# Weight tiles moved 64 bytes further on, and the second MLP's token shift taken out

## The chip, the cores and the metric

The kernel runs on one core of one Trainium2 chip. The metric is the device time of one execution in microseconds (us). Three runs of the kernel before gave 1178.79, 1179.38 and 1179.67 us, a median of 1179.38 us. All times below are of that kernel unless said otherwise.

A matmul on TensorE (PE) has two operands in SBUF. The *stationary* one (`lhsT`, 128 columns) is loaded into the array by a weight load (engine PEld in the profile); the *moving* one (`rhs`, here 256 or 512 columns) is then streamed through. The weight load of the next matmul runs while the present one streams.

## The reference

Two layers of a small diffusion transformer over 256 image tokens (x) and 256 context tokens (ctx), width 1024, all in float32. Layer 0 mixes tokens by retention (4 heads, keys 256 wide, values 512 wide, forward and backward), layer 1 by neighbourhood attention (32 heads of 32). Each is followed by a gated residual with a layer norm, and by an MLP:

```python
def sq_relu_mlp(h, w1, w2):
    return jnp.square(jax.nn.relu(h @ w1)) @ w2

h = x * (1.0 + sc2) + sh2
x = layer_norm(DN_ALPHA * x + g2 * sq_relu_mlp(h, mlp_w1[i], mlp_w2[i]), ln_g[i, 1], ln_b[i, 1])
```

`w1` is 1024x4096 and `w2` 4096x1024. In layer 0 the MLP is applied to image and context tokens, in layer 1 (the last) to the 256 image tokens alone. Shifts, scales and gates come from `c` and `c_ctx` by the 1024x6144 matrices `ada_w`.

## The kernel before, in words

**Three products for one.** Each float32 operand is split in a high part (rounded to the type that PE multiplies at one pass, `float32r`) and a low part (the rest). A product of two such pairs is three matmuls into one PSUM bank: high by high, high by low, low by high (`mm3`, line 174). So PE runs three matmuls per block, and nearly all of them have one of the weights' tiles, `hi` or `lo`, as an operand.

**Weights.** The list `specs` holds 228 blocks of weights (mostly 512 KB) in the order of use. `fetch` (line 255) loads a block into a `raw` tile with a DMA on SP's queue, ScalarE (ACT) rounds it into a `hi` tile, and VectorE (DVE) subtracts to make `lo`. `hi` tiles come from pool `hip` and `lo` tiles from pool `lop`, five of each. One block lies instead in an arena slot (tile `hilo`), and two in the pool of scratch tiles, `scp`.

**Tokens.** The normalised, scaled and shifted tokens stand transposed in `hTh` and `hTl` (high and low), 128 partitions by 8 blocks of 512 columns, image tokens first. `hs(k, a, b)` (line 583) gives columns a to b of block k of both.

**Which operand moves.** The places differ in what is loaded and what is streamed:

- Weights stationary, tokens moving. With 512 columns: retention's queries and keys (PSUM tile `pq`), the first MLP's first product (`p`, `mm1`, line 1254), part of the attention's keys (`pn`). With 256 columns: the first MLP's first two column blocks, where image and context tokens are taken apart (`p`); the attention's queries and the other part of its keys (`pn`, lines 1445 and 1475); and the second MLP's first product (`p`, `mm1` called at line 2072).
- Weights moving, the other operand stationary. With 512 columns: values (`pv`, `pnv`), gates (`pg`), the two output projections (`pw`, `pnw`), and the second products of both MLPs (`p<-hi,hid`, `p<-lo,hid`). With 256 columns: a quarter of the second MLP's second product (`mm2b`, line 2094), part of `pnw`, and the opening of the second MLP, where the tokens of one half come before the other's (`tok_part`, line 1975, PSUM tile `p1t`).
- No weights' tile at all: retention scores (`pS`), score times value (`po`), attention scores, transposes.

**Where the tiles lie.** SBUF is handed out pool by pool in the order in which the pools are opened (lines 136 to 142). By the built program, every large tile of the kernel before starts at 160 modulo 512 bytes of its partition: `hTh` at 40608, `raw` from 81568, `hi` from 97952, `lo` from 118432, scratch from 138912, the arena from 155296. Blocks within a tile are multiples of 512 bytes apart, so each operand of a matmul starts at 160 too, with one exception: in the second MLP the tokens are written, and read, 112 columns (448 bytes) further on in each block (`AT = 7 * LINE`, `LINE` being 16 floats). There the tokens' operand starts at 160 + 448 = 608, which is 96 modulo 512.

**What sets the order.** A scheduler orders the instructions of an engine, save where the code pins them (`keep_in_program_order`). All instructions are recorded through one helper, so the profile gives line 84 for nearly all of them; the tile names tell the place.

Of the kernel before, what the change touches and what calls it, by code (L numbers as in the profile page):

```python
# [10 lines left out]
F32 = mybir.dt.float32  # L11
# [6 lines left out]
P = 128  # L18
# [18 lines left out]
LINE = 16  # L37
# [67 lines left out]
def kernel(  # L105
# [27 lines left out]
    ec = ctx.enter_context  # L133
# [2 lines left out]
    smp = ec(tc.tile_pool(name="smp", bufs=4))  # L136
    cpool = ec(tc.tile_pool(name="cpool", bufs=1))
    rawp = ec(tc.tile_pool(name="rawp", bufs=4))
    hip = ec(tc.tile_pool(name="hip", bufs=WB))
    lop = ec(tc.tile_pool(name="lop", bufs=WB))  # L140
    scp = ec(tc.tile_pool(name="scp", bufs=8))
    arena = ec(tc.tile_pool(name="arena", bufs=1))
    dram = ec(tc.tile_pool(name="dram", bufs=1, space=DRAM))
    psp = ec(tc.tile_pool(name="psp", bufs=8, space=PSUM))

# [10 lines left out]
    def bank(s="ps"):  # L156
        return psp.tile([P, 512], F32, tag="ps", name=nm(s))

    def slot(i, shape, dt, s):

        return arena.tile(shape, dt, tag=f"s{i}", name=nm(s))
# [4 lines left out]
    def tsl(t):  # L166
        return slice(t * P, (t + 1) * P)
# [6 lines left out]
    def mm3(o, a, b, start, stop):  # L174
        (ah, al), (bh, bl) = a, b
        pe.matmul(o, lhsT=ah, rhs=bh, start=start, stop=False)
        pe.matmul(o, lhsT=ah, rhs=bl, start=False, stop=False)
        pe.matmul(o, lhsT=al, rhs=bh, start=False, stop=stop)
# [76 lines left out]
    def fetch(n, in_scratch=False, at=None):  # L255

        for src, k, ncol in specs[len(units) : len(units) + max(n, 0)]:
            raw = rawp.tile([P, k, ncol], F32, tag="raw", name=nm("raw"))
            sp.dma_start(out=raw[:], in_=src.rearrange("(k p) n -> p k n", p=P))
            if in_scratch or len(units) in scratch_units:  # L260
                hi, lo = Rows([scr("hi", F32R) for _ in range(k)]), Rows([scr("lo", F32R) for _ in range(k)])
                for i in range(k):
                    act.copy(out=hi[:, i, :], in_=raw[:, i, :])
                    pending.append((lo[:, i, :], raw[:, i, :], hi[:, i, :]))
                units.append((hi, lo))
                continue
            if at is None:
                hi = hip.tile([P, k, ncol], F32R, tag="hi", name=nm("hi"))
                lo = lop.tile([P, k, ncol], F32R, tag="lo", name=nm("lo"))
            else:  # L270
                both = slot(at, [P, 2, k, ncol], F32R, "hilo")
                hi, lo = both[:, 0], both[:, 1]
            act.copy(out=hi[:], in_=raw[:])
            pending.append((lo[:], raw[:], hi[:]))
            units.append((hi, lo))

    def lows(n=100, eng=None):
        for lo, raw, hi in pending[:n]:
            (eng or dve).tensor_sub(out=lo, in0=raw, in1=hi.bitcast(F32))
        del pending[:n]  # L280

    def take(n, ahead=WB, open_=0):
        first = taken[0]
        while len(units) < min(first + max(n, ahead), len(specs)):
            fetch(1)
            lows()
        taken[0] = first + n
        assert len(units) - len(pending) >= first + n - open_
        return units[first : first + n]
# [293 lines left out]
    def hs(k, a, b):  # L583
        return hTh[:, k, a:b], hTl[:, k, a:b]
# [108 lines left out]
    def residual(t, xn, gb, eng=None):  # L693
        if eng:
            eng.tensor_mul(out=R[t], in0=xn, in1=gb[:, 0, :])
            eng.tensor_add(out=R[t], in0=R[t], in1=gb[:, 1, :])
            return
        pool.on = True
        pool.tensor_mul(out=R[t], in0=xn, in1=gb[:, 0, :])
        pool.tensor_add(out=R[t], in0=R[t], in1=gb[:, 1, :])  # L700
        pool.on = False
# [303 lines left out]
    for h in range(RH):  # L1005
# [158 lines left out]
        if not last:  # L1164
            for half in range(2):
                us = take(2)
# [80 lines left out]
    def relu_sq(ps, sl, hh, hl):  # L1247
        split(squared(ps, sl), hh, hl)
# [3 lines left out]
    LAT, ALL, CTX = slice(0, NLAT), slice(0, NT), slice(NLAT, NT)  # L1252

    def mm1(us, sl, pb, ks=range(KC), at=0):
        for i in range(2):
            for k in ks:
                wh, wl = us[k // 4]
                mm3(
                    pb[i][:, sl], (wh[:, k % 4, tsl(i)], wl[:, k % 4, tsl(i)]),
                    hs(k, at + sl.start, at + sl.stop), k == 0, k == KC - 1,  # L1260
                )
# [15 lines left out]
    for hf in range(2):  # L1277
# [9 lines left out]
        if hf == 0:  # L1287
            us = take(2, 2, 1)
# [35 lines left out]
        for fp in range(len(hid), 8):  # L1324
            ht = hslot(fp)
            pb = [bank("p1") for _ in range(2)]
            us = take(2)
# [15 lines left out]
        for half in range(2):  # L1343
            last = hf == 1 and half == 1
            pb = [bank("p2") for _ in range(4)]
# [519 lines left out]
    us = take(2, 0)  # L1865
# [64 lines left out]

    AT = 7 * LINE
    ht = slot(N_Q, [P, 4, 2, NLAT], F32R, "hid1")
    us4 = take(2, 0, 1)

    def toks(t):
        return slice(AT + t * P, AT + (t + 1) * P)

    def affine_half(pts, half, t, on_act, eng=dve):  # L1940
        aff = mod_aff(pts[half], half, t, A, B, on_act)
        ks = slice(4 * half, 4 * half + 4)
        hi, lo = hTh[:, ks, toks(t)], hTl[:, ks, toks(t)]
        av_ = aff[:].rearrange("p (k t) -> p k t", k=4)
        act.copy(out=hi, in_=av_)
        return lambda: eng.tensor_sub(out=lo, in0=av_, in1=hi.bitcast(F32))

    def direct(pts, t):

        hi, lo = hTh[:, :, toks(t)], hTl[:, :, toks(t)]  # L1950
        tmps = [scr("aff") for _ in range(2)]

        def part(on_act, half, out_of):
            for i in range(4):
                k = 4 * half + i
                a, b = A[:, k, 0:1], B[:, k, 0:1]
                o, x_ = out_of(k, i), pts[half][:, tsl(i)]
                if on_act:
                    act.activation(out=o, in_=x_, func=AF.Identity, scale=a, bias=b)
                else:  # L1960
                    dve.tensor_scalar(out=o, in0=x_, scalar1=a, scalar2=b, op0=ALU.mult, op1=ALU.add)

        for half in range(2):
            part(half == 0, half, lambda k, i: hi[:, k])

        def low(half):
            part(True, half, lambda k, i: tmps[half][:, tsl(i)])
            ks = slice(4 * half, 4 * half + 4)
            dve.tensor_sub(
                out=lo[:, ks], in0=tmps[half][:].rearrange("p (k t) -> p k t", k=4), in1=hi[:, ks].bitcast(F32)  # L1970
            )

        return low

    def tok_part(ps, t, f2, a, b, ks=range(KC), start=False, stop=False):
        for k in ks:
            pe.matmul(
                ps[:, :256],
                lhsT=hs(k, toks(t).start, toks(t).stop)[a],
                rhs=us4[2 * f2 + k // 4][b][:, k % 4, :],  # L1980
                start=start and k == ks[0],
                stop=stop and k == ks[-1],
            )
# [7 lines left out]
    def turn_block(r, t, f2, ht=ht):  # L1991
        pt = bank("pt")
        for i in range(2):
            pe.transpose(pt[:, tsl(i)], r[:, tsl(i)], ident)
        src = pt[:, :256].rearrange("p (i t) -> p i t", i=2)
        hi, lo = (ht[:, 2 * f2 : 2 * f2 + 2, a, tsl(t)] for a in range(2))
        act.copy(out=hi, in_=src)
        dve.tensor_sub(out=lo, in0=src, in1=hi.bitcast(F32))
# [67 lines left out]
    for f4 in range(1, 8):  # L2066
        ht = slot(HS1[f4], [P, 4, 2, NLAT], F32R, "hid1")
        for f2 in range(2):
            opening = f4 == 1 and f2 == 0
            us = take(2, 0, 2) if opening else take(2)  # L2070
            pb = [bank("p1") for _ in range(2)]
            mm1(us, LAT, pb, at=AT)
            dve.on = f4 < 3
            for i in range(2):
                relu_sq(pb[i], LAT, ht[:, 2 * f2 + i, 0, :], ht[:, 2 * f2 + i, 1, :])
                if opening:
                    fetch(1)
                    lows(1)
                if opening and i == 0:
                    turn_block(r10, 1, 0, hid[0])  # L2080
                    turn_block(r11, 1, 1, hid[0])
            if opening:
                for e in (pe, act, pool):
                    e.on = False
        hid.append(ht)
        if f4 in (1, 2):
            residual(f4 - 1, xn2[:, f4 - 1, :], gb, dve)
        dve.on = False
# [125 lines left out]
```

## Time and profile before

| | |
|---|---|
| median of 3 runs | 1179.38 us (1178.79 to 1179.67) |
| the profiled execution's own time | 1179.48 us |
| its span | 1177.4 us |
| PE busy | 1167.3 us, 6821 matmuls |
| weight loads (PEld) busy | 985.6 us |
| DVE, ACT, POOL busy | 844.6, 480.6, 212.5 us |
| PE's granted clock, mean | 0.998 of full speed |

The matmuls are pipelined: one is shown as lasting longer than the distance to the next. So a busy time of PE says little, and what a matmul costs in a row of matmuls is the distance from its start to the next one's start, called its *step* below. It is read from the timeline (two starts and the number between them) or from a piece of the chain of work that ended last (its length by its count). The mean duration of a group of matmuls is the step and a constant on top, so that differences between two groups of like shape are differences of their steps.

### The profile page before, as it was taken

Reading aid. Unit: us, or ns where it says so; the run is one execution under the profiler, and the core shown is the slowest. Engines: PE = TensorE matmul, PEld = TensorE weight load, DVE = VectorE, ACT = ScalarE, POOL = GpSimd, SP = SyncE. Lnnn points to the kernel's source line nnn. Section 1 sums busy time; section 2 is a strip of 40 time slices with the busy share of each in tenths; the row PEclk is TensorE's granted clock in tenths of the full one; section 3 lists DMA queues with packets and bytes.
Section 4 is the critical chain, followed back from the end, with each engine's and each line's share of the span. In section 5 each row is a group of like instructions: output and inputs, shape, how many; then the busy total and the mean of one; then the engine's idle time right before and its main releaser. Section 6 shows DMA issues by size and latency. Waiting matters only on the chain.

```text
span 1177.4 us, 17745 instructions
## 1 busy us (share of the span) xinstructions
PE 1167.3 (99%) x6821; PEld 985.6 (84%) x6821; DVE 844.6 (72%) x1349; ACT 480.6 (41%) x819; POOL 212.5 (18%) x364
## 2 busy tenths in 40 slices
PE   9999999999999999999999999999999999999997
PEld 7788888888888889888888888889888878999886
DVE  3786678787888787757767675678577589877446
ACT  3643332222323246442212333137466666665341
POOL 0103001000200241780203000223343430000001
PEclk9999999999999999999999999999999999999999
DMA  9943544544355416757566665646344334766660
GB/s 276 276 130 104 161 143 140 152 147 152 118 169 175 141 60 214 189 112 217 171 190 197 212 199 190 201 141 204 83 135 139 111 115 155 222 209 197 233 212 36
DMA packets 140115, 195.10 MB, mean 166 GB/s; under 512 B 9936, under 2 KB 81136, under 8 KB 140032
## 3 DMA queue, kind: packets, MB, share of 16 engines
q1 hardware_dynamic: 131904, 182.03, 49.4%
q0 software_dynamic: 6976, 9.39, 3.9%
q10 hardware_dynamic: 1152, 2.56, 0.7%
q8 instruction: 53, 0.87, 0.3%
q14 instruction: 30, 0.25, 0.1%
HBM read 189.12 MB, written 5.75 MB: 166 GB/s over the span
## 4 chain that ended last, share of the span: by engine, by line
PE 94%; DMA 2%; SPq 1%; ACT 1%; DVE 1%; issue 0%; POOL 0%; ACTq 0%; DVEq 0%
PE p L84 44%; PE pw L84 7%; PE pg L84 7%; PE pq L84 7%; PE pv L84 7%; PE pn L84 5%; PE pnv L84 4%; PE po L84 3%; PE ppt L84 2%; PE pnw L84 1%; PE pS L84 1%; PE pav L84 1%; PE pqk L84 1%; SPq L84 1%; PE pt L84 1%; PE p1t L84 1%
## 5 line engine op out<-in xcount | busy, mean ns | idle before, releaser
L84 ACT CAST hi<-raw 128x1024 fp32r<-128x1024 f32 (+2 forms) x228 | 231.7, 1032 | 308.9 <-PE p L84 113.4
L84 DVE TENSOR_TENSOR lo<-raw,hi 128x1024 fp32r<-128x1024 f32 (+2 forms) x228 | 273.4, 1213 | 105.5 <-ACT hi L84 105.4
L84 PE MATMUL p<-hi,hid 128*128 128x512 f32 (+1 forms) x832 | 241.8, 373 | 0.0
L84 PEld LDWEIGHTS p<-hi,hid 128*128 128x128 f32 x832 | 152.1, 188 | 27.6
L84 PE MATMUL p<-hTh,lo 128*128 128x256 f32 (+1 forms) x512 | 165.8, 326 | 0.0
L84 PE MATMUL p<-hTl,hi 128*128 128x256 f32 (+1 forms) x512 | 165.8, 326 | 0.0
L84 PE MATMUL p<-hTh,hi 128*128 128x256 f32 (+1 forms) x512 | 162.9, 328 | 0.0
L84 PE MATMUL p<-lo,hid 128*128 128x512 f32 (+1 forms) x416 | 155.2, 373 | 0.0
L84 DVE SCALAR_TENSOR_TENSOR acc<-rawa,scol,acc 128x1024 f32<-128x1024 f32 x56 | 74.5, 1342 | 66.0 <-DMA rawa<-in_ada_w_dram 66.0
L84 PEld LDWEIGHTS p<-hTh,lo 128*128 128x128 f32 x512 | 96.4, 188 | 8.8
L84 PEld LDWEIGHTS p<-hTl,hi 128*128 128x128 f32 x512 | 96.4, 188 | 8.7
L84 PEld LDWEIGHTS p<-hTh,hi 128*128 128x128 f32 x512 | 94.2, 188 | 8.7
L84 PEld LDWEIGHTS p<-lo,hid 128*128 128x128 f32 x416 | 78.4, 188 | 13.7
L84 DVE SCALAR_TENSOR_TENSOR strips<-rawa,scol,strips 128x512 f32<-128x512 f32 x112 | 78.6, 762 | 0.0
L84 ACT CAST hid<-r 128x256 fp32r<-128x256 f32 (+1 forms) x64 | 31.9, 500 | 111.2 <-DVE r L84 111.2
L84 POOL TENSOR_TENSOR rstd<-rstd,misc 128x1 f32<-128x1 f32 x28 | 19.1, 684 | 212.4 <-DVE rstd L84 211.4
L84 POOL TENSOR_TENSOR R<-R,acc 128x512 f32<-128x512 f32 x16 | 25.8, 1633 | 168.8 <-DVE acc L84 168.8
L84 ACT ACTIVATE s<-s,mn 128x512 f32<-128x512 f32 x64 | 45.5, 713 | 22.0 <-DVE mn L84 22.0
L84 PE MATMUL pw<-hi,oh 128*128 128x512 f32 x128 | 51.0, 398 | 0.0
L84 PE MATMUL pg<-hi,hTh 128*128 128x512 f32 x128 | 50.6, 395 | 0.0
L84 PE MATMUL pq<-hTh,hi 128*128 128x512 f32 x128 | 49.3, 395 | 0.8 <-ACT hTh L84 0.5
L84 PE MATMUL pw<-hi,ol 128*128 128x512 f32 x128 | 49.9, 390 | 0.0
(238 smaller groups left out, 2278.5 us busy)
## 6 DMA issues: line engine op xcount, KB each, us to landing
raw<-in_mlp_w_dram SPq DMA_DIRECT2D x128, 512.0 KB, 4.2
rawa<-in_ada_w_dram SPq DMA_DIRECT2D x80, 512.0 KB, 3.9
raw<-in_ret_w_in_dram SPq DMA_DIRECT2D x42, 512.0 KB, 3.9
raw<-in_nat_w_in_dram SPq DMA_DIRECT2D x24, 512.0 KB, 4.3
rawq<-in_ada_w_dram SPq DMA_DIRECT2D x16, 512.0 KB, 6.2
raw<-in_ret_w_o_dram SPq DMA_DIRECT2D x16, 512.0 KB, 3.4
bias<-rpb_rows POOLq DMA_DIRECT2D x32, 128.0 KB, 2.9
raw<-in_nat_w_o_dram SPq DMA_DIRECT2D x8, 512.0 KB, 3.8
```

Source lines behind the costliest of these rows:

```text
L84: r = f(*args, **kwargs)
```

## The change

The pools of the scratch tiles and of the arena are opened ahead of those of the weights' tiles, and a 64-byte tile (`gap`) is put between. `hi` tiles now start from 188128 and `lo` tiles from 208608, both 224 modulo 512; scratch, arena, `raw`, `hTh` and `hTl` stay at 160. The three blocks that lie in the arena or in scratch tiles stay at 160 with them. The second MLP's tokens lose their shift and start at 160, like the tokens everywhere else.

With the distance of the stationary operand's start from the moving one's, modulo 512, as *offset*:

| matmuls | offset before | offset after |
|---|---|---|
| weights stationary, all places but the second MLP | 0 | +64 |
| weights stationary, second MLP (`mm1` at line 2072) | 160 - 96 = +64 | 224 - 160 = +64 |
| weights moving, all places but `tok_part` | 0 | -64 |
| weights moving, second MLP's `tok_part` | 96 - 160 = -64 | 160 - 224 = -64 |
| no weights' tile, and the three blocks elsewhere | 0 | 0 |

Instructions, their order on each of the five engines, and the semaphores that they wait for are the same in both programs, but for the numbers in names; only addresses differ.

```diff
     rawp = ec(tc.tile_pool(name="rawp", bufs=4))
+    scp = ec(tc.tile_pool(name="scp", bufs=8))
+    arena = ec(tc.tile_pool(name="arena", bufs=1))
+    apart = ec(tc.tile_pool(name="apart", bufs=1))
     hip = ec(tc.tile_pool(name="hip", bufs=WB))
     lop = ec(tc.tile_pool(name="lop", bufs=WB))
-    scp = ec(tc.tile_pool(name="scp", bufs=8))
-    arena = ec(tc.tile_pool(name="arena", bufs=1))
+    gap = apart.tile([P, 16], F32, tag="gap", name="gap")
...
-    AT = 7 * LINE
     ht = slot(N_Q, [P, 4, 2, NLAT], F32R, "hid1")
     us4 = take(2, 0, 1)
 
     def toks(t):
-        return slice(AT + t * P, AT + (t + 1) * P)
+        return slice(t * P, (t + 1) * P)
...
             pb = [bank("p1") for _ in range(2)]
-            mm1(us, LAT, pb, at=AT)
+            mm1(us, LAT, pb)
             dve.on = f4 < 3
```

## The prediction

> **What bounds the kernel now.** I read the page's first part and its chain of work that ended last, then the groups of matmuls by shape, then the chain in order of time and the timeline for steps.
>
> ```profile
> span 1177.4 us, 17745 instructions
> PE 1167.3 (99%) x6821; PEld 985.6 (84%) x6821; DVE 844.6 (72%) x1349; ACT 480.6 (41%) x819; POOL 212.5 (18%) x364
> PEclk9999999999999999999999999999999999999999
> PE 94%; DMA 2%; SPq 1%; ACT 1%; DVE 1%; issue 0%; POOL 0%; ACTq 0%; DVEq 0%
> ```
>
> PE stands in 94% of the chain at an undiminished clock, so a matmul that steps faster ends the kernel sooner, as long as its weights arrive. The profiled execution took 1179.48 us, 2.1 over its span and 0.1 over the median of the three runs; I start from 1179.4.
>
> The change removes, adds and reorders no instruction. What it can move is the step of matmuls whose two operands now start at another distance. So the step is read for each offset that the trace has. Columns here: start, length, what, count.
>
> ```profile
> 129.60 21.76 PE pq L84 x96
> 151.36 21.76 PE pv L84 x96
> 441.00 5.75 PE p L84 x48
> 796.52 5.75 PE pn L84 x48
> 803.14 14.53 PE pn L84 x120
> 996.06 8.03 PE p1t L84 x68
> ```
>
> At offset 0 a matmul of 512 columns steps 21.76/96 = 0.2267 us, whether weights are loaded (pq) or streamed (pv). One of 256 columns steps 5.75/48 = 0.1198 (p, pn). At offset -64, 256 columns (p1t) step 8.03/68 = 0.118. Timeline rows for offset 0 and 256 columns (pn), then for offset +64 (p, second MLP), each a few steps apart:
>
> ```profile
> 810.07 0.28 PE L84 MATMUL pn<-hTl,hi 128*128 128x256 f32 x1
> ...
> 810.79 0.28 PE L84 MATMUL pn<-hTl,hi 128*128 128x256 f32 x1
> ...
> 1012.00 0.28 PE L84 MATMUL p<-hTh,hi 128*128 128x256 f32 x1
> ...
> 1012.34 0.28 PE L84 MATMUL p<-hTh,hi 128*128 128x256 f32 x1
> ```
>
> The first pair is six steps: 0.72/6 = 0.120. The second is three: 0.34/3 = 0.1133. Shape, operands and order within a triple are the same; 6.7 ns apart. The form groups show that this isn't a matter of a few rows (the whole second MLP, asked for by its window, then the attention's queries and keys):
>
> ```profile
> L84 PE MATMUL p<-hTl,hi 128*128 128x256 f32 x208 | 57.4, 276 | 0.0
> ...
> L84 PE MATMUL pn<-hTl,hi 128*128 128x256 f32 x56 | 15.8, 283 | 0.0
> ```
>
> 276 against 283 ns: the same 7.
>
> **The change part by part: narrow matmuls, weights stationary, offset 0 to +64.**
>
> ```profile
> L84 PE MATMUL p<-hTl,hi 128*128 128x256 f32 x288 | 78.6, 278 | 0.0
> L84 PE MATMUL pn<-hTh,hi 128*128 128x256 f32 x96 | 27.5, 287 | 0.0
> ```
>
> Each group stands three times (one for each product). pn: 3 x 96 = 288. p: 3 x 288 = 864, of which 3 x 224 = 672 are the second MLP's, so 192 belong to the first MLP. 480 matmuls by 6.7 ns are 3.2 us. The first of a run already steps at 0.113 (below), so I take 3.0. All lie in PE pieces of the chain, end to end, so the gain is the kernel's. If it isn't, weights came late: the next limit in those stages is a raw tile's DMA and its rounding. The bounds are 0 and 3.2.
>
> **The second MLP's first product** goes from +64 to +64 by another way: 672 matmuls, no change. If the offset is not what counts, they lose 672 x 6.7 ns = 4.5 us (a rival below). The opening (p1t) stays at -64: no change.
>
> **Narrow matmuls, weights moving, offset 0 to -64.**
>
> ```profile
> L84 PE MATMUL p<-hi,hid 128*128 128x256 f32 x128 | 25.2, 282 | 0.0
> L84 PE MATMUL p<-lo,hid 128*128 128x256 f32 x64 | 18.1, 283 | 0.0
> ```
>
> 192, and 36 of pnw. At -64 the trace has 0.118 (p1t above, 68 of them) and also, in a first stretch, better:
>
> ```profile
> 991.17 0.62 PE L84 MATMUL p1t<-hi,hTh 128*128 128x256 f32 x4
> 991.62 0.62 PE L84 MATMUL p1t<-lo,hTh 128*128 128x256 f32 x4
> 992.07 1.59 PE L84 MATMUL p1t<-hi,hTh 128*128 128x256 f32 x9
> ```
>
> Eight steps from 991.17 to 992.07 are 0.90, so 0.1125 to 0.1135 each. So -64 has a good and a bad state, and after a pause PE stayed in the bad one. I take the commoner, 0.118: 228 x 2.2 ns = 0.5 us gained. Bounds: 0 and 228 x 6.7 = 1.5 us.
>
> **Wide matmuls: the open term.** None of 512 columns stands at another offset than 0. Counted from these rows:
>
> ```profile
> L84 PE MATMUL p<-hi,hid 128*128 128x512 f32 x704 | 221.0, 390 | 0.0
> L84 PE MATMUL p<-lo,hid 128*128 128x512 f32 x352 | 137.1, 390 | 0.0
> L84 PE MATMUL p<-hTh,hi 128*128 128x512 f32 x224 | 87.5, 391 | 0.0
> L84 PE MATMUL pw<-hi,oh 128*128 128x512 f32 x128 | 51.0, 398 | 0.0
> L84 PE MATMUL pg<-hi,hTh 128*128 128x512 f32 x128 | 50.6, 395 | 0.0
> L84 PE MATMUL pq<-hTh,hi 128*128 128x512 f32 x128 | 49.3, 395 | 0.8 <-ACT hTh L84 0.5 <-DVE hTh L84 0.4
> L84 PE MATMUL pv<-hi,hTh 128*128 128x512 f32 x128 | 46.1, 391 | 0.0
> L84 PE MATMUL pnv<-hi,hTh 128*128 128x512 f32 x64 | 25.7, 402 | 0.0
> L84 PE MATMUL pn<-hTh,hi 128*128 128x512 f32 x48 | 19.3, 402 | 0.0
> ```
>
> Weights moving: 704 + 352 + 3 x (128 + 128 + 128 + 64) = 2400, with some 66 of pnw 2466. Weights stationary: 3 x (224 + 128 + 48) = 1200. A nanosecond on each of these 3666 is 3.7 us, more than all the rest. What happens where widths meet tells most. In the second MLP's second product, one quarter pair has 256 columns (a row of two is two matmuls):
>
> ```profile
> 1084.66 0.39 PE L84 MATMUL p<-lo,hid 128*128 128x512 f32 x1
> 1084.89 0.50 PE L84 MATMUL p<-hi,hid 128*128 128x512 f32 x2
> 1085.23 0.28 PE L84 MATMUL p<-lo,hid 128*128 128x256 f32 x1
> 1085.35 0.40 PE L84 MATMUL p<-hi,hid 128*128 128x256 f32 x2
> ...
> 1086.78 0.40 PE L84 MATMUL p<-lo,hid 128*128 128x512 f32 x1
> 1087.02 0.62 PE L84 MATMUL p<-hi,hid 128*128 128x512 f32 x2
> 1087.48 0.39 PE L84 MATMUL p<-lo,hid 128*128 128x512 f32 x1
> ```
>
> 1084.89 to 1085.23 is one wide and one narrow matmul: 0.34 = 0.2267 + 0.1133. So the narrow one that follows wide ones steps at 0.1133 at offset 0; only the next go to 0.12. The other way round, the wide ones after narrow ones step 0.24, 0.23, 0.23, and then settle at 0.2267. And 0.2267 is twice 0.1133. I read this as a floor in proportion to the columns, on which a clash between the weight load and the stream adds up to 7 ns, depending on how far apart in time and address they run. Wide matmuls at offset 0 settle clear of it, narrow ones don't. At +64 narrow ones are clear as well, so wide ones should be: 0 for 1200. At -64 wide ones may settle clear (as they do at 0) or stay in the state of p1t. I take the floor, because a wide matmul leaves the weight load twice the time and settles even at the offset where narrow ones are worst. Bounds for the 2466: nothing gained or lost, to 4.8 ns each (p1t's 0.118 over 0.1133), 11.8 us lost; at 6.7 ns, 16.5 us.
>
> Sum: -3.0 - 0.5 = -3.5 us, 1175.9 us.
>
> A rule that speaks against the change: the Trainium skill, TensorE: Matmul & The Clock Gate, "Step-by-step: what each phase is for", says that PE reads SBUF through two independent ports and that loading the next weights takes no read bandwidth from the running matmul. By it no address could matter, and the sum would be 0. The steps of 0.120 and 0.1133 disagree; what would be left of it is the third rival.
>
> **The rivals.**
>
> *Wide matmuls with moving weights stay in the clash at -64.* For it: 68 matmuls of p1t did, at 0.118, though the first stretch did not. Against it: wide ones leave the clash at 0. Price 11.8 us, less the 3.5: 1179.4 + 8.3 = 1187.7. It decides from 3.5/2466 = 1.4 ns a matmul on. Chance 0.27.
>
> *The tokens' own place counts, not the offset.* Then the second MLP loses 4.5 us and nothing is gained: 1183.9. For it: no other moving operand starts at 96. Against it: the first stretch of p1t, streaming weights from 160, also stepped 0.1133. Chance 0.08.
>
> *Placement has no part,* and the second MLP steps faster for another reason of its stage: 1179.4. Against it are the narrow matmuls at 1085 us, 4 us behind that stage and back at 0.12. With gains and small losses that cancel: 0.08.
>
> *The wide ones gain too,* if 0.2267 is a clash and no floor. At 6.7 ns on 1200 and 2.2 to 6.7 on 2466: 13 to 25 us more, about 1157. Against it: the meeting rows. Chance 0.07. The same page's "Back-to-back issue gap" gives N/2.4 + 2.5 ns, 215.8 for 512 columns, 10.9 under the step here; no row of this trace comes near it.
>
> **How the numbers follow.** The likeliest case, -3.5 us, has 0.50; its own range is 1172 (all bounds good, and the wide ones' settling after pauses gone) to 1179. A difference under 0.2% (2.4 us) can't be told from none. Faster: nine tenths of 0.50 and the 0.07, 0.52. Slower: 0.27 + 0.08, 0.35. Same: the remaining 0.13. The range must reach into the first rival: 1171 to 1190 leaves out most of the last rival and the first one's far end.
>
> **What would show it.** pn and the first MLP's narrow groups fall from 283 to 276 ns, the second MLP stays at 276, the pieces x96 of pq and pv stay at 21.76 us. Wrong: pv, pg, pw or p<-hi,hid steps above 0.2267 in steady stretches; the second MLP at 283; or a wide step below 0.2267.

## The result, and the profile after

The changed kernel takes 1189.91 us (median of 6 runs, 1189.07 to 1194.38) against 1179.36 us for the kernel before in the same comparison: a ratio of 1.0093, with a 95% interval of 1.0081 to 1.0105. It is slower by 10.5 us; the prediction had 3.5 us faster. The profiled execution took 1189.45 us. Its first part, clock and chain shares:

```profile
span 1187.7 us, 17745 instructions
PE 1177.6 (99%) x6821; PEld 983.0 (83%) x6821; DVE 845.1 (71%) x1349; ACT 479.7 (40%) x819; POOL 212.7 (18%) x364
PEclk9999999999999999999999999999999999999999
PE 93%; ACT 2%; DVE 2%; DMA 1%; issue 1%; POOL 0%; ACTq 0%; DVEq 0%; POOLq 0%
```

The span has grown by 10.3 us (1187.7 against 1177.4), and PE's busy time by the same 10.3 (1177.6 against 1167.3), at the same clock and with the same 6821 matmuls. No other engine's busy time moved by more than 1 us except PEld, which fell by 2.6. So the loss should lie in the steps of the matmuls, and the sum further down bears this out. The chain in order of time (start, length, what, count):

```profile
113.14 16.48 PE pw L84 x72
129.63 22.39 PE pq L84 x96
152.02 22.39 PE pv L84 x96
...
179.03 11.00 PE pg L84 x48
...
817.32 10.94 PE pn L84 x94
...
1007.05 8.04 PE p1t L84 x68
```

`pq` and `pv` stood at 21.76 us for 96, 0.2267 each. Now they take 22.39, 0.2332 each: 6.6 ns more for a wide matmul, both with the weights stationary (`pq`, offset +64) and with the weights moving (`pv`, -64). `pg` and `pw`, also at -64, step 11.00/48 = 0.2292 and 16.48/72 = 0.2289. Narrow `pn` went from 0.121 (14.53/120) to 10.94/94 = 0.1164, and `p1t`, whose offset did not change, is where it was. The groups by shape say the same of the whole kernel:

```profile
L84 PE MATMUL p<-hi,hid 128*128 128x512 f32 x704 | 223.2, 393 | 0.0
L84 PE MATMUL p<-hTh,hi 128*128 128x512 f32 x224 | 88.8, 396 | 0.0
L84 PE MATMUL pq<-hTh,hi 128*128 128x512 f32 x128 | 49.9, 400 | 0.4 <-DVE hTh L84 0.4
L84 PE MATMUL pv<-hi,hTh 128*128 128x512 f32 x128 | 46.7, 396 | 0.0
L84 PE MATMUL pn<-hTl,hi 128*128 128x256 f32 x96 | 26.7, 278 | 0.0
L84 PE MATMUL p<-lo,hid 128*128 128x256 f32 x64 | 17.7, 277 | 0.0
```

The second MLP's first product, asked for by the window 1023 to 1083 us, is at 276 ns as before:

```profile
L84 PE MATMUL p<-hTl,hi 128*128 128x256 f32 x178 | 49.1, 276 | 0.0
```

Against before: the wide groups `p<-hi,hid`, `p<-hTh,hi`, `pq` and `pv` went from 390, 391, 395 and 391 ns to 393, 396, 400 and 396, and the narrow `pn<-hTl,hi` and `p<-lo,hid` from 283 and 283 to 278 and 277.

To add this up, I took from each timeline all distances from one matmul's start to the next one's, sorted them by class, and subtracted the floor (226.67 ns wide, 113.33 narrow). Distances more than 8% above the floor are waits and were left out (about a hundred of the 3666 wide ones). What is left is the excess of a class, in us. It is worked out from all rows of the traces; the columns on the right belong to experiments below.

| class (count) | before | after | `at0` | `wm64` | `arena64` | `w128` |
|---|---|---|---|---|---|---|
| wide, weights stationary (1200) | 0.5 | 7.7 | 0.5 | 2.9 | 0.6 | 7.0 |
| wide, weights moving (2466) | 1.9 | 8.0 | 1.9 | 15.7 | 4.7 | 14.5 |
| narrow, weights stationary, first MLP and attention (480) | 3.0 | 1.1 | 3.0 | 2.1 | 3.0 | 2.5 |
| narrow, second MLP's first product (672) | 0.0 | 0.0 | 4.4 | 0.0 | 0.2 | 0.0 |
| narrow, weights moving, `p<-hid` (192) | 1.2 | 0.2 | 1.2 | 0.7 | 0.0 | 0.8 |

After less before: +7.2 and +6.2 for the wide classes, -2.0 and -1.0 for the narrow ones, together +10.4. The span says 10.3.

### The profile page after: what moved, and what is told of

Its sections match the earlier page's. It is cut to its first block, busy times and chain, and to the rows that moved or that the text cites. A ratio compares the mean times of both kernels' runs of the same rounds, so it can differ in the third digit from the quotient of the medians.

```text
span 1187.7 us, 17745 instructions
## 1 busy us (share of the span) xinstructions
PE 1177.6 (99%) x6821; PEld 983.0 (83%) x6821; DVE 845.1 (71%) x1349; ACT 479.7 (40%) x819; POOL 212.7 (18%) x364
## 4 chain that ended last, share of the span: by engine, by line
PE 93%; ACT 2%; DVE 2%; DMA 1%; issue 1%; POOL 0%; ACTq 0%; DVEq 0%; POOLq 0%
PE p L84 43%; PE pq L84 8%; PE pv L84 8%; PE pw L84 7%; PE pg L84 7%; PE pnv L84 4%; PE po L84 3%; PE pn L84 2%; PE pnw L84 2%; PE pS L84 1%; PE ppt L84 1%; PE pada L84 1%; PE pav L84 1%; ACT s L84 1%; PE pt L84 1%
## 5 line engine op out<-in xcount | busy, mean ns | idle before, releaser
L84 PEld LDWEIGHTS p<-hTh,lo 128*128 128x128 f32 x512 | 96.2, 188 | 10.3
L84 PE MATMUL pg<-hi,hTl 128*128 128x512 f32 x128 | 50.2, 393 | 0.0
```

The lines of the kernel that those rows point to most:

```text
L84: r = f(*args, **kwargs)
```

## The experiments

The theory after the result: a matmul's step depends on the distance between the starts of its two operands, and wide matmuls are clear of the clash only at the offset that the kernel before had. The rivals: the place itself counts (behind all other tiles, or at 224), whatever the distance; the wide matmuls slow down because of something beside PE (rounding, DMAs); distance counts but not its sign.

### Place without distance

`behind` moves the weights' pools behind all others and leaves out the 64 bytes, so that all offsets are as before. `all64` puts 64 bytes ahead of every large tile, so that all stand at 224 and all offsets are as before. `at0` leaves the tiles alone and only takes the second MLP's shift out, so that its offset is 0.

```diff
     rawp = ec(tc.tile_pool(name="rawp", bufs=4))
-    hip = ec(tc.tile_pool(name="hip", bufs=WB))
-    lop = ec(tc.tile_pool(name="lop", bufs=WB))
     scp = ec(tc.tile_pool(name="scp", bufs=8))
     arena = ec(tc.tile_pool(name="arena", bufs=1))
+    hip = ec(tc.tile_pool(name="hip", bufs=WB))
+    lop = ec(tc.tile_pool(name="lop", bufs=WB))
```

> The kernel before with the pools of the weights' tiles opened last, as in the change, but without the 64-byte gap and with the second MLP's shift kept: every offset is as before. If the offset alone sets the steps, the time is that of before, 1179.4 us within 1.2. If it is the place behind all other tiles that costs, 1189.9. Half of each would be 1184.6.

```diff
     smp = ec(tc.tile_pool(name="smp", bufs=4))
+    apart = ec(tc.tile_pool(name="apart", bufs=1))
+    gap = apart.tile([P, 16], F32, tag="gap", name="gap")
     cpool = ec(tc.tile_pool(name="cpool", bufs=1))
```

> The kernel before with a 64-byte tile ahead of the constants, so that all large tiles, weights' and others', start at 224 modulo 512; the second MLP's shift is kept, so no offset changes. If only the distance between the two operands counts, 1179.4 us within 1.2. If a start at 224 modulo 512 is what costs (the weights' tiles stand there after the change), some of the 10.5 us are seen, at most all: 1189.9.

```diff
-    AT = 7 * LINE
+    AT = 0
```

> The kernel before with the second MLP's tokens not shifted: its 672 narrow matmuls go from offset +64 to 0 and the 96 of its opening from -64 to 0, nothing else moves. If the offset sets the steps, 672 x 6.7 ns = 4.5 us and 96 x 2 ns = 0.2 us are lost: 1184.1 us, and the group p<-hTl,hi of 256 columns in the second MLP goes from 276 to 283 ns. If the second MLP is fast for another reason of its stage, 1179.4.

`behind`: 1179.04 us, ratio 0.9997 (0.9988 to 1.0007). `all64`: 1179.12 us, 1.0001 (0.9992 to 1.0010). `at0`: 1183.33 us, 1.0035 (1.0022 to 1.0048), 4.3 us more than the kernel before in the same comparison (1179.06). The second MLP's groups in `at0`, asked for by the window 1023 to 1083 us:

```profile
L84 PE MATMUL p<-hTh,lo 128*128 128x256 f32 x168 | 47.5, 283 | 0.0
...
L84 PE MATMUL p<-hTl,hi 128*128 128x256 f32 x167 | 47.3, 283 | 0.0
```

The 276 ns of before have become 283, and the class's excess went from 0.0 to 4.4 us (672 x 6.6 ns). By the times, neither the place behind all tiles nor the start at 224 costs anything that can be measured, while taking the offset away does.

The offset does not settle everything, though. In the traces of `behind` and `all64`, whose executions took 1186.71 and 1182.29 us, the second MLP's first product steps 0.1178 us and not the 0.1133 of before, with the same offset of +64 and the same order of matmuls: 281 ns in place of 276 by shape, an excess of 3.0 us on the class. The second MLP's piece of the chain, in `all64` (162.12 in `behind` too, 159.33 before):

```profile
1010.53 162.12 PE p L84 x1104
```

(`behind` lost some 4 us more within its first 27 us, ahead of all the matmuls of the table.) Since the median times are those of before, this is not the price of the place: at +64 a narrow matmul has two steps, and something other than the offset and the order chooses, in all likelihood anew in each execution. The streams below show the same pair.

### Streams of matmuls by themselves

`micro` leaves the model out and runs streams of 40 matmuls on one pair of tiles, wide and narrow, at eleven offsets. Each offset is run twice: once straight behind a wide stream at offset 0 (names in f), once after a pause (names in p). While they run, the DMA engines are 1% busy, and DVE and ACT only drain finished streams.

```diff
+OFFSETS = (0, 16, 32, 48, 64, 128, 192, 256, 320, 384, 448)
...
+        for j in range(n):
+            s = off // 4 + P * (j % 16)
+            m = NT * (j % 4)
+            pe.matmul(
+                ps[:, :width],
+                lhsT=first if first is not None and j == 0 else sta[:, s : s + P],
+                rhs=mov[:, m : m + width],
...
+            ps = stream("z", 512, 0, 16)
+            ps = stream(w + "f" + letter, width, off, STREAM)
+            ps = stream(w + "p" + letter, width, off, STREAM, again[:])
```

> Not the model: all its work is left out, and the output isn't its result. Streams of 40 matmuls, each with its own weight load, operands a multiple of 512 bytes apart plus an offset: 512 columns (tiles wf, wp) and 256 columns (nf, np), entered straight from a wide stream at offset 0 (f) and after a pause (p); the last letter gives the offset of the stationary operand: a 0, b 16, c 32, d 48, e 64, f 128, g 192, h 256, i 320, j 384, k 448 bytes (448 is -64). If the offset sets the steps as in the two traces: narrow 0.120 at a, 0.1133 at e, 0.113 to 0.118 at k; wide 0.2267 at a, about 0.233 at e, 0.229 to 0.233 at k. If the wide matmuls of the changed kernel lose for a reason of the kernel (other engines, transfers, pauses), wide stays 0.2267 at all offsets here. Nothing of the two traces says what 16 to 48 and 128 to 384 give.

The groups by shape; the third letter counts the offsets (a is 0, b 16, e 64, f 128, h 256, i 320, k 448, which is -64):

```profile
L45 PE MATMUL wfi<-mov,sta 128*128 128x512 f32 x40 | 9.5, 395 | 0.0
...
L45 PE MATMUL wfe<-mov,sta 128*128 128x512 f32 x40 | 9.5, 395 | 0.0
...
L45 PE MATMUL wff<-mov,sta 128*128 128x512 f32 x40 | 9.5, 395 | 0.0
...
L45 PE MATMUL wfk<-mov,sta 128*128 128x512 f32 x40 | 9.3, 391 | 0.0
...
L45 PE MATMUL wfa<-mov,sta 128*128 128x512 f32 x40 | 9.3, 390 | 0.0
...
L45 PE MATMUL wfh<-mov,sta 128*128 128x512 f32 x40 | 9.2, 389 | 0.0
...
L45 PE MATMUL nfa<-mov,sta 128*128 128x256 f32 x40 | 5.0, 283 | 0.0
...
L45 PE MATMUL npk<-mov,sta 128*128 128x256 f32 x39 | 4.8, 279 | 0.0
L45 PE MATMUL npe<-mov,sta 128*128 128x256 f32 x39 | 4.6, 276 | 0.0
```

The durations are close to those of the model: 390 wide and 283 narrow at offset 0, 395 and 276 (after a pause) at +64, 391 and 279 at -64. Read as steps from start to start, once a stream is steady (ns):

| offset, bytes | wide | narrow |
|---|---|---|
| 0 and 256 | 226.67 | 120 |
| 16 | 226.67 or 233.33 | 118.3 |
| 32 and 48 | 233.33 | 118.3 |
| 64 and 320 | 233.33 | 113.33 or 117.8 |
| 128 and 384 | 232.4 | 118.5 or 120 |
| 192 and 448 (-64) | 228.89 | 117.8 |

Three things follow. The loss is PE's own: it is there with almost nothing else running. Each offset reads the same 256 bytes further on, so the period is 256 bytes where measured, not 512. And at offset 0, the best for wide matmuls, narrow ones are at their slowest. The two values of a cell belong to the two entries; `micro2` took that apart. It runs streams of 48 behind 24 matmuls of another width or offset (`b`):

```diff
+            drain(stream("b", width, off, 24, again[:]), width)
+        width, off = after
+        ps = stream(name, width, off, 48, None if before else again[:])
...
+        ("wb", (W, 0), (W, 448)),
+        ("wc", (W, 64), (W, 448)),
...
+        ("wi", (N, 64), (W, 0)),
...
+        ("nc", (N, 0), (N, 448)),
+        ("nd", (W, 0), (N, 448)),
...
+        ("ng", (W, 448), (N, 64)),
+        ("nh", (W, 0), (N, 64)),
```

> Not the model: all its work is left out, and the output isn't its result. Streams of 48 matmuls as in the first stream kernel, each after a stream of 24 of another width and offset, or after a pause. 512 columns at -64: wa after a pause, wb after wide 0, wc after wide +64, wd after narrow +64, we after narrow -64. 512 at 0: wg after wide +64, wh after narrow 0, wi after narrow +64, wj after wide -64. 256 at -64: na after a pause, nb after wide -64, nc after narrow 0, nd after wide 0, nj after wide +64. 256 at +64: ne after wide +64, ng after wide -64, nh after wide 0, ni after narrow 0. If a stream keeps the state in which it is entered: wa and wb 0.2289, wc 0.2333; nb and nc 0.1133 (as in the changed kernel's quarter and in p1t's first stretch), na and nd 0.1178; nh 0.1178. If each offset has one value: all of -64 alike, 0.2289 and 0.1178. Wide at 0 goes to 0.2267 from everywhere by both.

The chain in order of time:

```profile
29.03 11.00 PE wb L45 x48
...
46.52 11.21 PE wc L45 x48
...
122.94 10.92 PE wi L45 x48
...
134.75 5.51 PE b L45 x24
...
158.62 5.60 PE b L45 x24
...
164.22 5.67 PE nb L45 x48
...
173.65 5.46 PE nc L45 x48
...
185.50 5.66 PE nd L45 x48
...
209.73 5.47 PE ng L45 x48
...
221.59 5.67 PE nh L45 x48
```

Wide at -64 steps 11.00/48 = 0.2292 behind wide at 0, but 11.21/48 = 0.2335 behind wide at +64, and stays there for all 48. Narrow at -64 steps 0.1138 behind narrow at 0 and 0.1179 behind wide at 0; narrow at +64 0.1140 behind wide at -64 and 0.1181 behind wide at 0. Wide at 0 came to 226.67 ns from each of four entries (`wi` is one). So at -64 (at 16 too for wide ones, at +64 and 128 for narrow ones) a stream keeps one of two steps; a wide stream at 0 keeps one only, and wide at +64 was never seen at another than 0.2333.

What a stream was entered from goes with its step in these pairs, and in the changed kernel: `pv` follows `pq` (+64) without a pause and steps 0.2332 at -64, while `pg`, behind `pS` (offset 0), steps 0.2292 at the same -64. One guess was missed: a narrow stream at -64 behind a wide one at -64 (`nb`) stepped 0.118, though in the changed kernel the quarter behind such wide matmuls steps 0.1133 (six steps in 0.68 us):

```profile
1107.19 0.28 PE L84 MATMUL p<-lo,hid 128*128 128x256 f32 x1
...
1107.87 0.28 PE L84 MATMUL p<-lo,hid 128*128 128x256 f32 x1
```

The fence above has the difference: the wide stream ahead of `nb` (158.62) itself kept the longer of its two steps, 5.60/24 = 0.2333, while the same stream, begun after the same kind of pause, took 5.51/24 = 0.2296 elsewhere (134.75). So the entry matters by the step that it keeps and not only by its width and offset, and after a pause a stream can come to either. What chooses is left open; `behind` and `all64` above, and `wm64` below, show that width and offset of what ran ahead do not.

### Other offsets in the whole kernel

`wm64` swaps the signs: weights 64 bytes back, -64 where they are stationary and +64 where they move, the second MLP kept at +64. `arena64` moves only the arena (hidden tiles and others that stand against moving weights) 64 bytes back, which leaves every wide matmul with stationary weights at 0.

```diff
     smp = ec(tc.tile_pool(name="smp", bufs=4))
-    cpool = ec(tc.tile_pool(name="cpool", bufs=1))
-    rawp = ec(tc.tile_pool(name="rawp", bufs=4))
     hip = ec(tc.tile_pool(name="hip", bufs=WB))
     lop = ec(tc.tile_pool(name="lop", bufs=WB))
+    apart = ec(tc.tile_pool(name="apart", bufs=1))
+    gap = apart.tile([P, 24], F32, tag="gap", name="gap")
+    cpool = ec(tc.tile_pool(name="cpool", bufs=1))
+    rawp = ec(tc.tile_pool(name="rawp", bufs=4))
...
-    AT = 7 * LINE
+    AT = 6 * LINE
```

> The kernel before with the weights' tiles 64 bytes back instead of on (modulo 256), so that offsets are the mirror of the change's: -64 where weights are stationary, +64 where they move; the second MLP's shift is 384 bytes instead of 448, so that its own offsets stay +64 and -64. If the steps follow the offset with its sign, as the streams gave them: 2466 wide at +64 lose 6.7 ns, 16.4 us; 1200 wide at -64 lose 2.2 ns (2.7 us), or 6.7 ns (8.0 us) where they inherit the slow state from those ahead; narrow ones gain about 1.9 us: 1196.3 to 1201.6 us. If only the distance counts and not its sign, the price is the change's: 1189.9.

1193.40 us, ratio 1.0112 (1.0097 to 1.0127). Chain in order of time:

```profile
113.62 16.80 PE pw L84 x72
130.42 21.99 PE pq L84 x96
152.41 22.40 PE pv L84 x96
...
179.42 11.20 PE pg L84 x48
```

`pq`, now at -64, steps 0.2291, and `pv` and `pg`, now at +64, 0.2333. `pq` follows `pw` without a pause (113.62 + 16.80 = 130.42), and `pw`, at +64, steps 16.80/72 = 0.2333: the entry behind which `pv` of the changed kernel and `wc` kept 0.233 did not lead to it here. The classes of the table: weights stationary +2.4 us (2.0 ns each, where +64 cost 6.0), weights moving +13.8 us (5.6 ns each, where -64 cost 2.5). Both expectations missed the time. The one that sees distance alone falls, since swapping the signs swapped the prices; the one that sees the sign had the direction, but its time was 2.9 us too high at its near end.

```diff
     smp = ec(tc.tile_pool(name="smp", bufs=4))
+    arena = ec(tc.tile_pool(name="arena", bufs=1))
+    apart = ec(tc.tile_pool(name="apart", bufs=1))
+    gap = apart.tile([P, 24], F32, tag="gap", name="gap")
     cpool = ec(tc.tile_pool(name="cpool", bufs=1))
...
-    arena = ec(tc.tile_pool(name="arena", bufs=1))
```

> The kernel before with the arena alone moved, 64 bytes back from all other large tiles (modulo 256): -64 for the second products of both MLPs (1056 wide, 192 narrow) and the output projections (450 wide); weights against tokens stay at 0 and +64 as before. If the state of a wide stream at -64 is that in which it is entered, these come from wide ones at 0, so 0.2289: 1506 x 2.2 ns = 3.3 us lost, 1.1 us gained by the narrow ones, 1181.3. If -64 costs 6.7 ns whatever came before: 10.0 - 1.1, 1188.0. If only weights against tokens count: 1179.1.

1180.24 us, ratio 1.0015 (1.0002 to 1.0027). Groups by shape:

```profile
L84 PE MATMUL p<-hi,hid 128*128 128x512 f32 x704 | 221.8, 391 | 0.0
...
L84 PE MATMUL p<-lo,hid 128*128 128x256 f32 x64 | 17.7, 276 | 0.0
```

The wide ones lost a nanosecond (390 to 391), the narrow quarter gained seven (283 to 276): +2.8 us on the class of the one (1.9 ns on each of the 1506 that moved), -1.2 on the other. The time lies between the two nearest expectations, 1.1 us from each; the class table speaks for the first, since the wide ones moved, and by far less than the 1188.0 needs. A good narrow step and a good wide step do not stand at one offset here either.

`w256` and `w128` test the streams' table where the model had not been: the weights 256 and 128 bytes back. In `w128` the second MLP's shift is set so that it stays at +64.

```diff
     smp = ec(tc.tile_pool(name="smp", bufs=4))
-    cpool = ec(tc.tile_pool(name="cpool", bufs=1))
-    rawp = ec(tc.tile_pool(name="rawp", bufs=4))
     hip = ec(tc.tile_pool(name="hip", bufs=WB))
     lop = ec(tc.tile_pool(name="lop", bufs=WB))
+    apart = ec(tc.tile_pool(name="apart", bufs=1))
+    gap = apart.tile([P, 72], F32, tag="gap", name="gap")
+    cpool = ec(tc.tile_pool(name="cpool", bufs=1))
+    rawp = ec(tc.tile_pool(name="rawp", bufs=4))
```

> The weights' pools stand first, 256 bytes behind the others modulo 512; the second MLP's shift stays. Offsets: -256 and 256 where the kernel before has 0, and -192 in the second MLP (which is +64 modulo 256). Theory, what counts is the offset modulo 256, as in the streams: no step changes, 1179.4, within 0.2%. Rival, the model's matmuls go by the offset modulo 512: the second MLP's narrow ones lose their clear step, 672 x 6.7 ns = 4.5 us, 1183.9, and more if the wide ones aren't clear at 256.

1179.22 us, ratio 0.9998 (0.9988 to 1.0009), as the period of 256 bytes has it. The second MLP, at -192 there, has the same groups as at +64 (window 1023 to 1083 us):

```profile
L84 PE MATMUL p<-hTh,lo 128*128 128x256 f32 x178 | 49.2, 276 | 0.0
```

For `w128`, the same but for two numbers:

```diff
-    gap = apart.tile([P, 72], F32, tag="gap", name="gap")
+    gap = apart.tile([P, 40], F32, tag="gap", name="gap")
...
-    AT = 7 * LINE
+    AT = 1 * LINE
```

> The weights 128 bytes behind the others modulo 256, and the second MLP's shift set so that it stays at +64 there. So all other matmuls with a weights' tile stand at 128, where the sign of the offset has no meaning. Theory, the streams' steps hold in the model: the 3666 wide ones go from 226.67 to 232.8 ns, 6.1 x 3666 = 22.4 us, and the narrow ones stay at 118.6 to 120 (0 to -0.7 us): 1201 to 1202. Rival, what a matmul is entered from keeps a part of them clear, as in the changed kernel (9.9... of 3666 x 6.6 = 24 us, 13.4 were lost): some 55% of it, 12.3 us, 1191.7. Rival, distance alone with its worst at 64: less than 12 us.

1196.70 us, ratio 1.0145 (1.0128 to 1.0162).

```profile
L84 PE MATMUL p<-hi,hid 128*128 128x512 f32 x704 | 224.8, 396 | 0.0
...
L84 PE MATMUL p<-hTh,hi 128*128 128x512 f32 x224 | 88.8, 396 | 0.0
L84 PE MATMUL pw<-lo,oh 128*128 128x512 f32 x128 | 50.5, 394 | 0.0
```

All wide groups slow down, whichever operand moves: +6.5 us on the 1200 and +12.6 on the 2466, 5.4 and 5.1 ns each. The streams' steps hold in kind, and both rivals fall: the one by which nearly half would stay clear (1191.7) and the one of distance alone (less than 12 us; the loss is 17.3). The time was 4 us under the expectation because I charged 6.1 ns to all 3666 (the 232.8 in the expectation is a little high, the steady streams give 232.4, which is 5.7 ns): about a hundred of them stand at waits, the others had some excess already (2.4 us in the table), and the narrow classes gave back 0.9.

### A version that uses it

The offset that is best for wide matmuls makes narrow ones 6.7 ns slow, so `wide13b` keeps every offset and replaces narrow matmuls by wide ones: the second MLP's last quarter pair is computed 512 wide for the first 13 units, added up, and split only for the last three. 156 narrow matmuls become 78 wide ones.

```diff
-    parts = {(t, half): [(bank("p2"), FULL)] for t, half in ((0, 0), (0, 1), (1, 0))}
-    parts[1, 1] = [(bank("p2"), slice(256 * q, 256 * q + 256)) for q in range(2)]
+    parts = {(t, half): [(bank("p2"), FULL)] for t in range(2) for half in range(2)}
+    group = {(t, half): (0, 31) for t in range(2) for half in range(2)}
+    group[1, 1] = (0, 25)
...
+    add_to(1, 1, gated(parts[1, 1][0][0], 1, 1, G2), dve)
+    parts[1, 1] = [(bank("p2"), slice(256 * q, 256 * q + 256)) for q in range(2)]
+    group[1, 1] = (26, 31)
```

> A version meant to beat the kernel before, all offsets as before: the quarter of the second MLP's second product that ran as 256-column halves runs as whole 512-column matmuls for the first 13 weight blocks, its sum is added to the residual once, and only the last 3 blocks are in halves. 156 narrow matmuls at 0.120 become 78 wide at 0.2267: 18.7 - 17.7 = 1.0 us, and 13 changes of width with 28 ns of settling each go: 0.4 us. 1177.7 us. If the extra addition on VectorE delays the end: up to 1.3 us back, 1179.1.

1178.52 us, ratio 0.9994 (0.9981 to 1.0006): 0.8 us over the expected 1177.7, and the interval holds no change. The second MLP's piece of the chain, before and then in `wide13b`:

```profile
1010.45 159.33 PE p L84 x1104
```

```profile
1010.70 158.05 PE p L84 x1026
```

It is 1.3 us shorter in this one profile, about what 156 narrow steps over the floor are worth (156 x 6.7 ns = 1.0), but too little to tell in the time. Five of its 12 executions (1177.45 to 1177.85 us) lie under the fastest of 23 of the kernel before (1178.40), and the other seven between 1178.41 and 1184.41. No version was found that beats the kernel before by a difference that can be measured.

## Why the prediction was wrong

**The time.** 1175.9 was predicted and 1189.9 came: inside the range by 0.1 us, on the other side of before. That it lies inside is luck: the upper end was set for the first rival, which held only half of the cause. The sum was -3.5 us of narrow gains and nothing for the wide; measured were -3.0 and +13.4.

**The step that failed** is the one on wide matmuls with stationary weights: "At +64 narrow ones are clear as well, so wide ones should be: 0 for 1200." They lost 7.2 us, 6.0 ns each, over half of the loss. The offset that is clear for narrow matmuls is the one at which wide streams never stepped under 233.33 in `micro`. In these runs the step of one width at an offset did not tell that of the other; I had carried it over because 0.2267 is twice 0.1133 and I read both as one floor, with one clash on top that the offset lifts for both. What the trace of before did have was a warning and not a proof: wide ones behind narrow ones stepped 0.24 and 0.23 before they settled, at an offset where, as `micro2` showed, a wide stream has but one step to settle at.

**The second half of the same step,** "I take the floor" for 2466 at -64, failed too: 6.2 us lost, 2.5 ns each, within the bounds given (0 to 11.8). Its reason was that a wide matmul leaves the weight load twice the time and settles at 0. Most settled at 0.229, and `pv`, behind `pq`, at 0.2332. Settling at 0 was no evidence for settling elsewhere.

**The rivals.** The first one gave 1187.7, 2.2 us from the result, and its mechanism (moving weights stay in the clash) is half of what happened, at half the price that it named. No rival held the other half, stationary weights at +64. The tokens' own place is out (in the changed kernel tokens at 160 keep the second MLP at 276 ns), and so is the case that placement has no part (`at0`). That the wide ones gain too is out: no stream in `micro` stepped under 226.67 or 113.33 at any offset.

**What was right.** The second MLP's 672 matmuls and `p1t` did not move (0.0 us and 8.04 us). The narrow groups gained: those with stationary weights 2.0 us in place of 3.0, because a part of them keeps the longer step of +64 (0.1164 on average in the `pn` piece, where 0.1133 was taken); those with moving weights 1.0 in place of 0.5, since they came to the shorter step of -64 and not the commoner one. That a step goes by offset and not by place, and that 226.67 and 113.33 are a floor, held in the runs; that an offset can have two steps was read from `p1t`, and was taken into the bounds at -64 alone, not at +64.

**The rule that was weighed.** The Trainium skill, TensorE: Matmul & The Clock Gate, "Step-by-step: what each phase is for", has two independent read ports, so that the load of the next weights takes no read bandwidth from the running matmul. By it the addresses could not matter. Here they do: with the addresses alone changed, the step in the streams went from 226.67 to 233.33 ns, and `w128` lost 17.3 us. That it is the load that costs this is not shown.

## What to carry to other kernels

A change of address can slow a PE-bound kernel with no instruction moved: look at the start of both operands of every matmul modulo 256 bytes, and read the step of each width at each offset from the trace or from a stream of 40 matmuls before placing tiles, behind more than one kind of entry, since a stream can have two steps at one offset. A width that was never seen at an offset is unknown there; with 3666 matmuls a nanosecond on each outweighs the gain on all the rest, so measure that term first. In this kernel, of the offsets tried, 0 is right for 512 columns and +64 for 256, and since the wide ones are five in seven of those with a weights' tile, the shift belongs to the one stage that has only narrow ones.

## What the runs showed of the hardware

- With both operands `float32r`, the best step at full clock was 226.67 ns for 512 columns and 113.33 for 256, at every offset that reached it.
- The offset of the two operands' starts adds 0, 2.2, 5.7 or 6.7 ns to a wide matmul and 0, 4.4, 5.0 to 5.2 or 6.7 to a narrow one; 256 bytes further on the same values came again (`micro`, `w256`). The sign counts: -64, by the shorter of its two steps, and +64 differ by 4.4 ns on a wide one.
- At some offsets a steady stream keeps one of two steps, over 48 matmuls at least (`wb` and `wc`). Width and offset of what ran ahead don't decide which: the same program part with the same offsets stepped 0.1133 or 0.1178 in different runs (the second MLP before, and in `behind` and `all64`: 2.8 us on its piece).
- That a weight load and a stream meet in SBUF is one reading of this. It wasn't shown: no run had the streams without loads.
